# Cached attention of a decoder layer: two decoded rows share the 128 partitions, and one matmul sums the scores of both

## The chip, the cores and the metric

The kernel runs on one core of one Trainium2 chip. The metric is the device time in microseconds (us), the median over several executions. The engines named below are PE (TensorE, matmuls), DVE (VectorE), ACT (ScalarE), POOL (GpSimd) and SP (SyncE, which here only issues loads of weights). Each engine works through its own list of instructions in order and waits on semaphores for the others.

## The reference

One layer of a hybrid decoder is computed for a prompt of 256 tokens and for 8 decoded rows (`DEC_BATCH` 8, one token each). It projects the normalised input (RG-LRU and mLSTM heads), adds cross attention over 256 memory tokens in 4 heads of 512 features, and adds a SwiGLU block. The change is in the cross attention of the 8 decoded rows. Their keys and values are not computed but come from a cache:

```python
xq = (rmsnorm(x, g_xa) @ w_xa_q).reshape(B, L, XA_HEADS, XA_DH)
s = jnp.einsum('blhd,bmhd->bhlm', xq, mk.astype(dt)).astype(jnp.float32) * (XA_DH ** -0.5)
p = jax.nn.softmax(s, axis=-1).astype(dt)
o = jnp.einsum('bhlm,bmhd->blhd', p, mv.astype(dt)).reshape(B, L, D_MODEL)
x = x + o @ w_xa_o
...
xs, st_s = layer(xs, ..., cache_mem_k[l], cache_mem_v[l], *w)
```

For each of the 4 heads and each of the 8 rows this is a product of one query of 512 features with 256 cached keys, a softmax over the 256 scores, and a weighted sum of 256 cached values: 32 pairs of head and row, each with 512 KB of keys and 512 KB of values.

## The kernel before

**Layout.** Features lie on the 128 partitions, tokens along the free axis: 264 columns, 256 of the prompt and 8 decoded. A product with a weight matrix is a step of the list `steps`: SP loads the weights of the step (512 KB per half step) into `raw`, ACT rounds them to a high half, DVE subtracts to get the low half (`split_half`, tile `w`), and PE adds three products of halves (`mm3`). The program has 41 steps for `w_in`, 16 for `w_out`, 16 for `w_q` (queries), 32 for `w_k` and `w_v` (keys and values of the prompt, eight per head), 16 for `w_o` and then the SwiGLU block. Tile `w` has four buffers, which is two steps.

**Side work.** What is not a projection is written as generators (`side`, `pump`). After each step the main loop lets them issue instructions until estimates of the busy time of DVE and ACT reach that of PE. The order in which the instructions then stand on PE, DVE, ACT and POOL is set by a scheduler from priorities and a model of time; the splits of the weights have high priority. At run time the order on each engine is fixed.

**Cached attention before.** `evac_q` (line 1123) writes the queries of the decoded rows to `qsm`, partition by feature. When the fourth query step is evacuated, it starts two generators. `dec_k` (line 1142) goes over heads and rows. For each row POOL issues two loads of 512 KB from `kcT` and `vcT` into buffers of the pool `B` (26 buffers, lines 1151 and 1155). ACT multiplies the first quarter of the keys with the query column, DVE adds the other three with `scalar_tensor_tensor`, into the accumulator `dw`. ACT rounds the sum to `ds[0]` and POOL subtracts to get `ds[1]` (line 1162). At most two rows are under way (`NFL`). `dec_v` (line 1166) sums over the partitions with two matmuls whose weights are a 128x128 tile of ones (`onesr`), so that each partition gets the whole score row. DVE takes the maximum, ACT the exponential with its sum, and DVE multiplies the four quarters of the values with the probabilities and sums each (`accum_out` into `osm`). After 8 rows of a head DVE scales `osm`, and `attend` (line 1264) may use it: ACT and DVE split it into the tail columns of the operand of `w_o`.

**Order of the work.** The loads of keys and values, the subtractions on POOL and the stores of the prompt's keys and values share POOL's one list. The first step of `w_o` (`pe_o`) needs both generators to be done.

## Time and profile before

| what | us |
|---|---|
| median of 3 runs (1456.42 to 1458.74) | 1457.74 |
| the profiled execution, its own time | 1455.83 |
| its span, from first to last instruction | 1454.1 |
| PE busy in the span | 1439.2 |
| DVE busy | 1045.1 |
| ACT busy | 794.9 |
| POOL busy | 128.3 |

The query steps and the cached attention lie between about 375 and 652 us of the span. Busy shares are means over the span, and DVE's differs much between stages. The prediction reads that stretch by itself.

### The profile page before, as it was taken

What the parts mean: (1) busy time and instruction counts of PE and PEld (TensorE: products, weight loads), DVE (VectorE), ACT (ScalarE), POOL (GpSimd) and SP (SyncE); (2) the same over time, 40 slices, a digit from 0 to 9 for tenths busy, and PEclk for the clock granted to TensorE, in tenths of its full rate; (3) what the DMA queues carried; (4) which work ended last, traced back from release to release, by engine and by line L of the source; (5) the groups of instructions that cost most, each with busy time, mean ns of one, the idle gap of its engine ahead of it and who ended that gap; (6) DMA issues with size and microseconds to landing.
All of it is one profiled execution on the core that took longest, in us unless ns stands there. A gap on an engine that the chain in (4) does not pass through costs nothing.

```text
span 1454.1 us, 30126 instructions
## 1 busy us (share of the span) xinstructions
PE 1439.2 (99%) x12071; PEld 1415.5 (97%) x12071; DVE 1045.1 (72%) x1999; ACT 794.9 (55%) x1279; POOL 128.3 (9%) x204
## 2 busy tenths in 40 slices
PE   9999999999999999999999999999999999999997
PEld 8999999999999999999999999999999999999997
DVE  7966797898899999987675666555665655565564
ACT  7678685666556666655544444434444443444463
POOL 0001210000124343410000000000000000000000
PEclk9999999999999999999999999999999999999999
DMA  9645896557799877955555555555555555555563
GB/s 288 234 171 179 268 363 231 177 178 271 254 344 355 340 284 297 375 172 192 197 195 194 197 193 201 190 202 190 198 194 196 196 198 194 195 197 192 172 195 112
DMA packets 99757, 326.02 MB, mean 224 GB/s; under 512 B 10944, under 2 KB 19824, under 8 KB 99616
## 3 DMA queue, kind: packets, MB, share of 16 engines
q1 hardware_dynamic: 83616, 269.84, 52.8%
q0 software_dynamic: 15136, 53.16, 10.2%
q8 instruction: 94, 1.54, 0.4%
q10 hardware_dynamic: 864, 1.09, 0.2%
q14 instruction: 47, 0.39, 0.1%
HBM read 312.78 MB, written 11.28 MB: 223 GB/s over the span
## 4 chain that ended last, share of the span: by engine, by line
PE 94%; ACT 2%; DMA 1%; DVE 1%; issue 1%; SPq 0%; POOL 0%; DVEq 0%; POOLq 0%
PE mm L60 90%; PE ax L60 5%; DMA raw<-w_in 1%; ACT B L60 1%; DVE B L60 1%; DMA B<-scr 0%; ACT w L60 0%; DVE w L60 0%; ACT L60 0%; SPq L213 0%; ACT dw L60 0%; DVE ds L60 0%; SPq L1412 0%; DMA scr<-lt 0%; ACT t L60 0%
## 5 line engine op out<-in xcount | busy, mean ns | idle before, releaser
L60 PE MATMUL mm<-B,w 128*128 128x264 f32 (+1 forms) x10960 | 1281.2, 279 | 2.5 <-DVE w L60 2.1
L60 PEld LDWEIGHTS mm<-B,w 128*128 128x128 f32 x10960 | 1260.6, 189 | 10.7 <-DVE w L60 2.4
L60 DVE TENSOR_TENSOR w<-raw,w 128x1024 fp32r<-128x1024 f32 (+1 forms) x522 | 625.4, 1200 | 312.9 <-ACT w L60 312.2
L60 ACT ACTIVATE w<-raw 128x1024 fp32r<-128x1024 f32 (+1 forms) x522 | 536.0, 1028 | 531.8 <-PE mm L60 370.8
L60 PE MATMUL mm<-w,B 128*128 128x512 f32 x384 | 86.5, 380 | 0.0
L60 PEld LDWEIGHTS mm<-w,B 128*128 128x128 f32 x384 | 70.7, 189 | 9.4
L1494 POOL TENSOR_TENSOR B<-B,rstd 128x264 f32<-128x264 f32 x4 | 2.8, 741 | 802.8 <-ACT rstd L60 802.8
L60 DVE TENSOR_TENSOR t<-mm,rstd 128x264 f32<-128x264 f32 x96 | 41.4, 432 | 28.8 <-PE mm L60 28.7
L60 DVE SCALAR_TENSOR_TENSOR B<-B,dw 128x256 f32<-128x256 f32 x128 | 52.2, 461 | 3.2 <-ACT dw L60 2.9
L60 DVE TENSOR_TENSOR xres<-xres,mm 128x264 f32<-128x264 f32 (+1 forms) x81 | 34.2, 424 | 27.2 <-PE mm L60 27.1
L60 DVE SCALAR_TENSOR_TENSOR dw<-B,qsm,dw 128x256 f32<-128x256 f32 x96 | 48.6, 512 | 0.8
L60 PE MATMUL ax<-B,B 128*128 128x256 f32 (+3 forms) x288 | 46.0, 302 | 0.8 <-DVE B L60 0.8
L1162 POOL TENSOR_TENSOR ds<-dw,ds 128x256 fp32r<-128x256 f32 x32 | 36.8, 1151 | 106.9 <-ACT ds L60 104.7
L60 PEld LDWEIGHTS ax<-B,B 128*128 128x128 f32 x288 | 39.9, 191 | 3.0 <-DVE B L60 1.0
L60 ACT ACTIVATE B<-xres,vecs 128x264 fp32r<-128x264 f32 (+1 forms) x64 | 32.1, 502 | 3.5 <-DVE xres L60 1.6
L60 ACT ACTIVATE t<-xres 128x264 f32<-128x264 f32 (+1 forms) x53 | 21.0, 409 | 16.0 <-DVE xres L60 16.0
L1151 POOL DMA_DIRECT2D B<-kcT x32 | 17.4, 544 | 122.8 <-DVE B L60 109.7
L60 DVE SCALAR_TENSOR_TENSOR B<-xres,vecs,B 128x264 fp32r<-128x264 f32 x48 | 23.3, 488 | 4.3 <-ACT B L60 4.3
L60 ACT ACTIVATE dw<-B,qsm 128x256 f32<-128x256 f32 x32 | 16.2, 507 | 16.3 <-issue 6.4
L60 ACT ACTIVATE B<-t 128x264 fp32r<-128x264 f32 (+1 forms) x60 | 24.1, 409 | 1.7 <-DVE t L60 1.5
L60 ACT ACTIVATE dw<-B,B 128x128 f32<-128x128 f32 x64 | 20.9, 390 | 7.1 <-DMA B<-scr 6.3
L60 ACT ACTIVATE dw<-ax,dw 128x256 f32<-128x256 f32 x32 | 15.0, 470 | 17.7 <-DVE dw L60 14.0
(172 smaller groups left out, 691.2 us busy)
## 6 DMA issues: line engine op xcount, KB each, us to landing
raw<-w_gu SPq DMA_DIRECT2D x176, 512.0 KB, 3.6
raw<-w_d SPq DMA_DIRECT2D x80, 512.0 KB, 3.7
raw<-w_in SPq DMA_DIRECT2D x74, 512.0 KB, 5.2
raw<-w_out SPq DMA_DIRECT2D x32, 512.0 KB, 3.8
B<-kcT POOLq DMA_DIRECT2D x32, 512.0 KB, 8.2
raw<-w_q SPq DMA_DIRECT2D x32, 512.0 KB, 5.4
B<-vcT POOLq DMA_DIRECT2D x32, 512.0 KB, 9.1
raw<-w_k SPq DMA_DIRECT2D x32, 512.0 KB, 5.1
```

What stands on the lines that cost most here:

```text
L60: return f(*a, **k)
L1151: pool_e.dma_start(kc, kcT[h, b])
L1162: pool_e.tensor_sub(ws[:, 1], acc, ws[:, 0].bitcast(F32))
L1494: e.tensor_mul(st["y"](c), st["y"](c), r)
```

## The change

Two decoded rows now share the partitions: partitions 0 to 63 hold one row, 64 to 127 the other. The 128 partitions of the former layout do not fit 64, so the even and the odd features of each 128-block lie in two tiles. A load takes every second partition line of two rows of `kcT`, 128 lines of 4 KB as before, and writes all partitions. The keys of a pair of rows are two tiles, the values too.

- `onesr` becomes block diagonal: ones in the two 64x64 blocks, zero elsewhere. One pair of matmuls then sums the scores of two rows, each over its own half.
- Per pair of rows there are one ACT product and seven DVE products for the keys, one rounding, one subtraction, one pair of matmuls, one maximum, one exponential and eight products for the values.
- The tiles of keys and values come from a `Ring` of two buffers each. The load of the next tile stands behind the fourth product with the tile whose buffer it takes.
- `swap_q` brings the queries of a head into the new layout: a copy on POOL into `q3`, and four copies by DMA within SBUF into `q2`. `swap_o` takes the result back the same way, into `osm`. The loads of the four heads make 32 such small DMAs.

```diff
@@ -1129,70 +1129,123 @@
             dve.tensor_mul(qn["t"](j)[:, m:T], p2[:, 1, : T - m], rstd[:, m:T])
             dve.tensor_mul(qsm[:, j, :], p2[:, 1, T - m:], rstd[:, T:N])
             qn["n"] = j + 1
+            if j % 4 == 3:
+                swap_q(j // 4)
             if j == 3:
                 with tc.issue_after(st["split"].ins):
-                    act.activation(onesr, ones, AF.Copy)
+                    act.activation(onesr, ones, AF.Copy, scale=0.0)
+                    for part in (LOW, HIGH):
+                        act.activation(onesr[part, part], ones[part, part], AF.Copy)
                 st["dk"] = side(dec_k(), 5)
                 st["dv"] = side(dec_v(), 4)
         return f
 
     pairs = []
     infl = {"n": 0}
+    NB2 = NS // 2
+    q2 = const.tile([P, H, 2, 4, NB2], F32, name="q2")
+    q3 = const.tile([P, 2, 2, 4, NB2], F32, name="q3")
+    o2, o3 = q2, q3
+    LOW, HIGH = slice(0, 64), slice(64, P)
+
+    by_row = lambda x: x.rearrange("p c (b s) -> p s c b", s=2)
+
+    def swap_q(h):
+        pool_e.tensor_copy(q3[:, h % 2], by_row(qsm[:, 4 * h: 4 * h + 4, :]))
+        for q, part in enumerate((LOW, HIGH)):
+            for e in range(2):
+                pool_e.dma_start(q2[part, h, e], q3[e: P: 2, h % 2, q])
+
+    def swap_o(h):
+        rec = ssm[:, h, 0: NB2]
+        dve.reciprocal(rec, rec)
+        o = o2[:, h].rearrange("p g c b -> p (g c) b")
+        dve.tensor_mul(o, o, rec.rearrange("p (c b) -> p c b", c=1).to_broadcast([P, 8, NB2]))
+        for q, part in enumerate((LOW, HIGH)):
+            for e in range(2):
+                pool_e.dma_start(o3[e: P: 2, h % 2, q], o2[part, h, e])
+        pool_e.tensor_copy(by_row(osm[:, 4 * h: 4 * h + 4, :]), o3[:, h % 2])
+
+    class Ring:
+        def __init__(self, src):
+            self.t, self.at = [B([P, 4, T]), B([P, 4, T])], 0
+            self.src = src.rearrange("h b p c t -> h (b p) c t")
+            self.load()
+            self.load()
+
+        def load(self):
+            u = self.at
+            if u < H * NB2 * 2:
+                self.at = u + 1
+                b = u // 2 % NB2 * 2 * P + u % 2
+                pool_e.dma_start(self.t[u % 2], self.src[u // NS, b: b + 2 * P - 1: 2])
+
+        def __call__(self, j):
+            return self.t[j // 4][:, j % 4, :]
 
     def dec_k():
+        kr = Ring(kcT)
+        st["vr"] = Ring(vcT)
+        yield STEP
         for h in range(H):
             while qn["n"] < 4 * h + 4:
                 yield STEP
-            for b in range(NS):
+            for b in range(NB2):
                 while infl["n"] >= NFL:
                     yield STEP
                 infl["n"] += 1
-                kc = B([P, 4, T])
-                pool_e.dma_start(kc, kcT[h, b])
                 w = sb.tile([P, 264], F32, tag="dw", bufs=2, name=nm("dw"))
                 ws = sb.tile([P, 2, T], F32R, tag="ds", bufs=2, name=nm("ds"))
-                vc = B([P, 4, T])
-                pool_e.dma_start(vc, vcT[h, b])
                 acc = w[:, 0:T]
-                q = [qsm[:, 4 * h + c, b: b + 1] for c in range(4)]
-                act.activation(acc, kc[:, 0, :], AF.Copy, scale=q[0])
-                for c in range(1, 4):
-                    dve.scalar_tensor_tensor(acc, kc[:, c, :], q[c], acc, op0=OP.mult, op1=OP.add)
+                for j in range(8):
+                    q = q2[:, h, j // 4, j % 4, b: b + 1]
+                    if j == 0:
+                        act.activation(acc, kr(0), AF.Copy, scale=q)
+                    else:
+                        dve.scalar_tensor_tensor(acc, kr(j), q, acc, op0=OP.mult, op1=OP.add)
+                    if j % 4 == 3:
+                        kr.load()
+                    if j == 3:
+                        yield 1.0
                 act.activation(ws[:, 0], acc, AF.Copy)
                 pool_e.tensor_sub(ws[:, 1], acc, ws[:, 0].bitcast(F32))
-                pairs.append((h, b, w, vc, ws))
+                pairs.append((h, b, w, ws))
                 yield 1.1
 
     def dec_v():
         done, cur = 0, None
-        while done < H * NS:
+        while done < H * NB2:
             nxt = None
             if pairs:
                 nxt = pairs.pop(0)
                 ps = bank("ax")
-                pe.matmul(by2(ps[:, :T]), onesr, turn(nxt[4][:, 0]), start=True, stop=False)
-                pe.matmul(by2(ps[:, :T]), onesr, turn(nxt[4][:, 1]), start=False, stop=True)
+                pe.matmul(by2(ps[:, :T]), onesr, turn(nxt[3][:, 0]), start=True, stop=False)
+                pe.matmul(by2(ps[:, :T]), onesr, turn(nxt[3][:, 1]), start=False, stop=True)
                 nxt += (ps,)
             cur, todo = nxt, cur
             if todo is None:
                 yield STEP
                 continue
-            h, b, w, vc, _, ps = todo
+            h, b, w, _, ps = todo
             mx, p = w[:, T: T + 1], w[:, :T]
             dve.tensor_reduce(mx, ps[:, :T], axis=AX.X, op=OP.max)
             dve.tensor_scalar(mx, mx, -XSCALE, None, op0=OP.mult)
             act.activation(halves(p), unturn(ps[:, :T]), AF.Exp, scale=XSCALE, bias=mx,
                            accum_out=ssm[:, h, b: b + 1])
             yield 0.5
-            for c in range(4):
-                dve.scalar_tensor_tensor(vc[:, c, :], vc[:, c, :], 1.0, p, op0=OP.mult, op1=OP.mult,
-                                         accum_out=osm[:, 4 * h + c, b: b + 1])
+            for j in range(8):
+                v = st["vr"](j)
+                dve.scalar_tensor_tensor(v, v, 1.0, p, op0=OP.mult, op1=OP.mult,
+                                         accum_out=o2[:, h, j // 4, j % 4, b: b + 1])
+                if j % 4 == 3:
+                    st["vr"].load()
+                if j == 3:
+                    yield 1.0
             infl["n"] -= 1
             done += 1
-            if done % NS == 0:
-                dve.reciprocal(ssm[:, h, :], ssm[:, h, :])
-                for c in range(4):
-                    dve.tensor_mul(osm[:, 4 * h + c, :], osm[:, 4 * h + c, :], ssm[:, h, :])
+            if done % NB2 == 0:
+                swap_o(h)
+                yield STEP
                 st["dh"] = h + 1
             yield STEP
 
```

**What moves.** Three places are shown, one on POOL and two on DVE. Names carry buffer numbers here.

POOL before, in the query steps: `ds` is the rounded score sum, `B_...` the tiles of keys (`kcT`) and values (`vcT`) of one row.

```order
L1162 TENSOR_TENSOR ds_633_5239<-dw_632_5238,ds_633_5239 128x256
L1151 DMA B_648_5386<-kcT 128x1024
L1155 DMA B_651_5390<-vcT 128x1024
L1151 DMA B_658_5470<-kcT 128x1024
L1155 DMA B_661_5474<-vcT 128x1024
L1151 DMA B_668_5554<-kcT 128x1024
L1155 DMA B_671_5558<-vcT 128x1024
L1162 TENSOR_TENSOR ds_650_5389<-dw_649_5388,ds_650_5389 128x256
```

The loads of three rows, into six different buffers, stand ahead of the next subtraction.

POOL now, in the same steps: `B_627` and `B_628` are the two buffers of the key ring (even and odd features), `B_629` and `B_630` those of the value ring.

```order
L1181 DMA B_627_5233<-kcT 128x1024
L1181 DMA B_629_5237<-vcT 128x1024
L1181 DMA B_630_5238<-vcT 128x1024
L1181 DMA B_628_5234<-kcT 128x1024
L1211 TENSOR_TENSOR ds_654_5476<-dw_653_5475,ds_654_5476 128x256
L1181 DMA B_627_5233<-kcT 128x1024
L1154 COPY q3_116<-qsm_112 128x32
L1157 DMA q2_115<-q3_116 64x16 x4
L1181 DMA B_628_5234<-kcT 128x1024
L1211 TENSOR_TENSOR ds_667_5633<-dw_666_5632,ds_667_5633 128x256
```

Each load goes into a buffer that was just read, and the small DMAs of `swap_q` stand between loads.

DVE now, the third and the fourth pair of rows: `dw_653` and `dw_666` are their accumulators, `w_...` the splits of weights, `B_660` and `qsm` the evacuation of a query step.

```order
L60 SCALAR_TENSOR_TENSOR dw_653_5475<-B_628_5234,q2_115,dw_653_5475 128x256
L60 TENSOR_TENSOR B_660_5562<-mm_670_5648,rstd_94 128x132
L60 TENSOR_TENSOR B_660_5562<-mm_670_5648,rstd_94 128x124
L60 TENSOR_TENSOR qsm_112<-mm_670_5648,rstd_94 128x8
L60 SCALAR_TENSOR_TENSOR dw_666_5632<-B_627_5233,q2_115,dw_666_5632 128x256
L60 TENSOR_TENSOR w_675_5717<-raw_665_5623,w_675_5717 128x8x128
L60 TENSOR_TENSOR w_682_5804<-raw_671_5697,w_682_5804 128x8x128
L60 SCALAR_TENSOR_TENSOR dw_666_5632<-B_628_5234,q2_115,dw_666_5632 128x256
```

The first row is the last read of the odd key tile for one pair, the last row its first read for the next pair. The load of that tile has to be issued and to land in between, while DVE has six instructions to do.

DVE now, the last two pairs of the fourth head, in the steps for the prompt's keys and values: `dw_849` and `dw_878` are their accumulators.

```order
L60 SCALAR_TENSOR_TENSOR dw_849_7250<-B_628_5234,q2_115,dw_849_7250 128x256
L60 TENSOR_TENSOR w_910_7723<-raw_900_7632,w_910_7723 128x1024
L60 SCALAR_TENSOR_TENSOR dw_878_7475<-B_627_5233,q2_115,dw_878_7475 128x256
L60 TENSOR_TENSOR w_918_7776<-raw_904_7698,w_918_7776 128x1024
L60 SCALAR_TENSOR_TENSOR dw_878_7475<-B_628_5234,q2_115,dw_878_7475 128x256 x2
```

Again the odd key tile is read for the last time in the first row and for the next pair in the last, with three instructions between.

## The prediction

> **What bounds the kernel now.** I read the engines' busy time first, then the busy time of the stretch that the change touches, then what PE waited for, then the groups and the order in time inside the stretch.
>
> ```profile
> PE 1439.2 (99%) x12071; PEld 1415.5 (97%) x12071; DVE 1045.1 (72%) x1999; ACT 794.9 (55%) x1279; POOL 128.3 (9%) x204
> ...
> 380.00:640.00 260.00, 260.00 (x1730) 242.96 (x1729) 248.74 (x639) 164.50 (x306) 95.55 (x130) 1.00 0.85 317
> 400.00:420.00 20.00, 20.00 (x181) 20.00 (x180) 19.64 (x58) 11.14 (x19) 5.78 (x10) 1.00 0.90 338
> 800.00:900.00 100.00, 100.00 (x892) 100.00 (x891) 60.20 (x74) 44.83 (x55) 0.00 (x0) 1.00 0.56 195
> ...
> PE mm L60 <- DVE w L60: 2.1, 2, 1.9
> PE ax L60 <- ACT w L60: 2.1, 3, 1.5
> ```
>
> The rows of stretches give, after the length, the busy us of PE, weight loads, DVE, ACT and POOL, then the granted clock, the DMA share and GB/s. PE is busy for all of 380 to 640 us at full clock, and DVE for 248.74 of 260, so DVE has only 11.3 us to spare there. A busy PE might still be paced by others, because the ends of matmuls are modelled. So I count: 181 matmuls in 20 us while the cached attention runs, against 892 in 100 us, or 178 in 20, in the SwiGLU block, where DVE is 60% busy. PE is not held back. In the whole run PE waited 2.1 us at most for any one partner; asked for 380 to 655 us alone, the view has no row. The kernel is therefore bound by PE, and DVE is close behind just here. A gain has to take matmuls away; work taken from ACT or POOL gains nothing by itself.
>
> **What the change takes away.**
>
> ```profile
> L60 PE MATMUL ax<-ds,onesr 128*128 128x256 f32 x64 | 17.1, 277 | 0.0
> L60 DVE SCALAR_TENSOR_TENSOR dw<-B,qsm,dw 128x256 f32<-128x256 f32 x96 | 48.6, 512 | 0.8
> L60 DVE SCALAR_TENSOR_TENSOR B<-B,dw 128x256 f32<-128x256 f32 x128 | 52.2, 461 | 3.2 <-ACT dw L60 2.9
> L1162 POOL TENSOR_TENSOR ds<-dw,ds 128x256 fp32r<-128x256 f32 x32 | 36.8, 1151 | 106.9 <-ACT ds L60 104.7 <-PE mm L60 2.0
> L60 ACT ACTIVATE dw<-B,qsm 128x256 f32<-128x256 f32 x32 | 16.2, 507 | 16.3 <-issue 6.4 <-DVE B L60 4.7 <-ACT w L60 2.9
> L60 DVE TENSOR_REDUCE dw<-ax 128x1 f32<-128x256 f32 x32 | 13.3, 416 | 0.3 <-PE ax L60 0.2
> L60 DVE TENSOR_SCALAR dw<-dw 128x1 f32<-128x1 f32 x32 | 4.7, 147 | 0.2
> ...
> 444.18 0.27 PE L60 MATMUL ax<-ds,onesr 128*128 128x256 f32 x1
> 444.29 3.17 PE L60 MATMUL mm<-B,w 128*128 128x264 f32 x23
> ...
> 394.83 1.22 DVE L60 TENSOR_TENSOR w<-raw,w 128x1024 fp32r<-128x1024 f32 x1
> 395.97 0.48 DVE L60 SCALAR_TENSOR_TENSOR dw<-B,qsm,dw 128x256 f32<-128x256 f32 x1
> 396.37 0.48 DVE L60 TENSOR_TENSOR B<-mm,rstd 128x132 f32<-128x132 f32 x2
> 396.76 0.15 DVE L60 TENSOR_TENSOR qsm<-mm,rstd 128x8 f32<-128x8 f32 x1
> 396.84 0.47 DVE L60 SCALAR_TENSOR_TENSOR dw<-B,qsm,dw 128x256 f32<-128x256 f32 x1
> 397.23 0.41 DVE L60 TENSOR_REDUCE dw<-ax 128x1 f32<-128x256 f32 x1
> ```
>
> The groups give count, busy us and mean ns, then idle time before them. PE loses 32 of the 64 matmuls on `onesr`. One lasts 277 ns but matmuls overlap: the next starts 0.11 us later (444.18 to 444.29). That is 32 x 0.11 = **3.5 us**, all on the path that sets the end. PE had no wait in the stretch, so no more than this can be won.
>
> DVE's instructions overlap too, so I use distances of starts: 1.14 us for a split of weights (394.83 to 395.97), 0.40 for a key product, 0.47 for an evacuation of queries with `qsm` (396.37 to 396.84), 0.33 for a maximum by the same reading. DVE gets 16 key products more (+6.4 us), and loses 16 maxima and 16 small scalings (16 x (0.33 + 0.15) = -7.7 us) and 12 small products on `osm`, at most 12 x 0.15 = -1.8. That is 3 us less, and none of it on the path. ACT loses 16 products of 0.507 us and 16 roundings and exponentials; PE never waited for it there, so it counts nothing. POOL loses 16 subtractions, 16 x 1.151 = 18.4 us, also off the path. But it may let DVE run faster: key products average 512 ns against 470 to 480 in the rows above, so 96 x 0.035 = 3.4 us, and the value products and splits look alike. I take 5 us of DVE time for half of POOL's subtractions gone, between 0 and 10. So DVE has 11.3 + 3 + 5 = 19 us to spare over the stretch.
>
> [...]
>
> **What it adds: hops through DMA.** `swap_q` is a copy on POOL, four DMA issues and their landing; `swap_o` the same backwards.
>
> ```profile
> L1494 POOL TENSOR_TENSOR B<-B,rstd 128x264 f32<-128x264 f32 x4 | 2.8, 741 | 802.8 <-ACT rstd L60 802.8
> scr<-lt POOLq DMA_DIRECT2D x1, 32.0 KB, 1.8
> o_h<-hlast POOLq DMA_DIRECT2D x1, 36.0 KB, 6.0
> 386.64 0.53 POOL L1151 DMA_DIRECT2D B<-kcT  x1
> 381.49 1.06 POOL L1162 TENSOR_TENSOR ds<-dw,ds 128x256 fp32r<-128x256 f32 x1 [25.96 <-ACT ds L60]
> 390.19 0.38 PE L60 MATMUL ax<-ds,onesr 128*128 128x256 f32 x2
> L60 DVE TENSOR_TENSOR osm<-osm,ssm x16: 151/156/164, 445.9 to 637.1; 128x8 f32<-128x8 f32 x16
> L60 DVE TENSOR_TENSOR B<-osm,B x16: 154/160/164, 533.3 to 652.0; 128x8 fp32r<-128x8 f32 x16
> ```
>
> A hop takes at most 0.74 + 4 x 0.53 + landing of 1.8 to 6.0, so 4.7 to 8.9 us. The first head's `swap_q` is covered by PE's own order: before, the first pair of halves was ready at 382.55 (381.49 + 1.06) and used at 390.19, 7.6 us later. The later heads' hops run while the head before is worked on. `swap_o` is covered by the distance from `osm` to its use, 14.9 us at the last head (637.1 to 652.0). Price if the cover is gone: 8.9 - 7.6 = 1.3 us once. I take 0.
>
> **What it adds: loads that cannot run ahead.** Before, POOL issued the loads of three rows at once into free buffers. Now a tile is loaded only when it has been read, and DVE, which holds the splits of weights, waits in order if it is late.
>
> ```profile
> DMA to landing us min/median/max: 3.8/8.2/13.9
> B<-kcT POOLq DMA_DIRECT2D x1, 512.0 KB, 4.6
> B<-kcT POOLq DMA_DIRECT2D x1, 512.0 KB, 4.0
> B<-kcT POOLq DMA_DIRECT2D x1, 512.0 KB, 6.1
> B<-kcT POOLq DMA_DIRECT2D x1, 512.0 KB, 13.9
> 414.48 0.88 POOL L1162 TENSOR_TENSOR ds<-dw,ds 128x256 fp32r<-128x256 f32 x1
> 417.07 0.27 PE L60 MATMUL ax<-ds,onesr 128*128 128x256 f32 x1
> 419.98 0.74 POOL L1162 TENSOR_TENSOR ds<-dw,ds 128x256 fp32r<-128x256 f32 x1
> 422.24 0.27 PE L60 MATMUL ax<-ds,onesr 128*128 128x256 f32 x1
> ```
>
> The first row is the time from issue to landing of the 32 key loads. The next are single ones, issued at 336.65, 429.72, 385.55 and 387.68 us: 4.0 to 6.1 with none of their own kind ahead, 13.9 as the fifth of a burst of six. The ring sends one or two at a time, so I take 5.0, nearest to the single ones, with 3.8 and 8.2 as ends.
>
> Against it stands DVE's work between the last read of a tile and the next. At the fourth pair of the order shown that is 0.47 + 0.40 + 2 x 1.14 = 3.2 us, so DVE waits 1.8 us. At the last pair it is 2 x 1.14 + 0.40 = 2.7 us, a wait of 2.3. Added up in the same way, the 15 gaps of the odd key tile are 4.0, 11.6, 3.2, 8.3, 8.7, 6.6, 6.5, 5.6, 7.7, 5.0, 9.3, 5.7, 5.7, 14.8 and 2.7; those of the even one have only one (4.4) below 5, those of the values none. With 5.0 DVE waits about 1.0 + 1.8 + 2.3 = 5.1 us, well inside the 19 us, so the weights do not run dry. But behind the waiting product stand the accumulator, its rounding on ACT, POOL's subtraction and the two matmuls, in PE's fixed order. Before, PE came to the second of these 1.7 and 1.5 us after POOL had ended (415.36 to 417.07, 420.72 to 422.24). With 1.5 us of slack, PE loses 0 + 0.3 + 0.8 = **1.1 us**.
>
> The sum against the profiled execution's 1455.83 us: -3.5 + 1.1 = -2.4, so 1453.4. The median of the runs is 1.9 above that execution; I carry the difference over: 1457.74 - 2.4 = **1455.3 us**, 0.16% less.
>
> **The rivals.**
>
> *No wait at all.* If loads land in about the shortest time seen, 3.8 us, the waits are 0.6 and 1.1 at two places, below the slack, and the whole 3.5 us remains: 1454.2. For it: the DMA engines are less pressed without bursts. Against: one load of the four single ones took 6.1. [...] The trace has no key load below 3.8.
>
> *The ring is too short.* If landings stay at their median of 8.2, the odd key tile alone is late ten times, by 4.2 + 5.0 + 1.6 + 1.7 + 2.6 + 0.5 + 3.2 + 2.5 + 2.5 + 5.5 = 29.3 us. DVE can make up 18 to 19, so PE runs dry of weights for about 11 us: 1457.74 - 3.5 + 11 = 1465 us, slower than before. At 7.0 the sum is 18 us, just what DVE can make up, so this mechanism decides from a mean landing of about 7 us on. For it: the DMA share of 0.85 in the stretch, and SP's weights go on beside it. Against: half of that pressure was the bursts.
>
> *The freed time goes elsewhere.* The matmuls are gone, but the first hop is late by 1.3 us, or PE is paced by DVE after all: 1456 to 1457.7. The count of matmuls above speaks against it.
>
> **How the numbers follow.** Forecast 0.38 (its own range 1454.2 to 1457.5), no wait 0.20, ring too short 0.32, time gone elsewhere 0.10. A change below 0.2%, 2.9 us, can hardly be told from none here, so faster means under 1454.8 and slower above 1460.7. Faster: 0.20 and 0.14 of the forecast's 0.38. Slower: 0.30 of the 0.32. The rest, 0.36, is between. Eight times in ten the time should lie from 1453.7, just under the whole gain, to 1466, just over the price of late loads.
>
> **What would show it.** Right: 32 matmuls on `onesr`, no wait of PE between 380 and 655 us above 1 us, key loads landing in about 5 us, short idle times of DVE or ACT before key products that name the load, DVE below 248 us of 260. Wrong: idle times of DVE that name key loads adding up to more than 19 us, PE waiting for `w`, or idle time of PE before matmuls on `onesr` of several us.

## The result, and the profile after

The changed kernel takes **1483.39 us** in the median of 4 runs (1480.59 to 1484.29), against 1457.55 for the kernel before beside it: a ratio of 1.0176, with a 95% interval of 1.0164 to 1.0189. I had forecast 1455.3 and a range up to 1466. The change costs some 26 us. The profiled execution took 1484.29 us, with a span of 1482.6. Two executions far outside the others are left out everywhere, one of the run with half of the bytes (1659.93 us, at a granted clock of 0.849) and one of the kernel before (3078.39 us).

First the engines' busy time on the page of the changed kernel, then the same three stretches as before and three short ones. After the length stand the busy us of PE, weight loads, DVE, ACT and POOL, the granted clock, the DMA share and GB/s:

```profile
PE 1445.4 (97%) x12039; PEld 1416.0 (96%) x12039; DVE 1046.6 (71%) x1971; ACT 772.9 (52%) x1217; POOL 133.1 (9%) x228
```

```profile
380.00:640.00 260.00, 237.19 (x1537) 216.63 (x1536) 229.59 (x577) 127.25 (x219) 93.66 (x145) 0.99 0.86 292
400.00:420.00 20.00, 20.00 (x181) 20.00 (x180) 19.33 (x61) 9.38 (x13) 6.90 (x12) 1.00 0.94 299
800.00:900.00 100.00, 100.00 (x891) 100.00 (x890) 61.33 (x76) 45.20 (x57) 0.00 (x0) 1.00 0.60 195
560.00:580.00 20.00, 14.19 (x87) 12.69 (x87) 15.48 (x42) 10.62 (x22) 6.55 (x12) 0.96 0.76 267
580.00:600.00 20.00, 20.00 (x109) 17.89 (x108) 19.13 (x41) 10.64 (x23) 10.50 (x17) 0.96 0.93 317
620.00:640.00 20.00, 16.10 (x93) 14.31 (x92) 15.71 (x45) 8.41 (x20) 6.86 (x9) 0.91 0.67 207
```

The 32 matmuls are gone (12071 to 12039), and the SwiGLU stretch is as it was. The loss lies where the cached attention runs: PE, busy for all of 380 to 640 us before, is now idle for 22.8 of the 260. DVE has no more to do than before (1046.6 us in the whole span against 1045.1), but within these 260 us it gets less of it done, 229.59 us against 248.74: it waits as well. Next, what PE waited for between 380 and 655 us (total us, times, longest); before, this view had no row:

```profile
PE ax L60 <- ACT ds L60: 6.5, 7, 1.8
PE mm L60 <- DVE w L60: 5.9, 3, 4.2
PE mm L60 <- DVE t L60: 3.9, 1, 3.9
PE ax L60 <- POOL ds L1211: 3.4, 4, 1.6
PE ax L60 <- DVE B L60: 1.7, 1, 1.7
PE ax L60 <- DVE dw L60: 1.3, 1, 1.3
```

The rows add up to 22.7 us. Most of them stand for two things: PE comes to the matmuls on `onesr` before their operand `ds` is ready (9.9 us), and the weights `w` come too late (5.9 us). The waits for `t` and `dw` (5.2 us) come right after waits of DVE for key loads, of 5.54 us until 623.25 and of 2.44 us until 538.03; the one for `B` (1.7 us) I did not trace. PE's idle time over the whole span grew by 22.3 us (from 14.9 to 37.2). Its busy time grew too, by 6.2 us with 32 matmuls fewer; the lower clock that was granted gives some 3 us of that by my estimate (last section), and the rest stays open. The waits lead back to one place, as the groups on the page show (busy, mean ns, then idle time and what ended it):

```profile
L60 DVE SCALAR_TENSOR_TENSOR dw<-B,q,dw 128x256 f32<-128x256 f32 x112 | 58.0, 522 | 25.0 <-DMA B<-kcT 19.8
L60 DVE SCALAR_TENSOR_TENSOR B<-B,dw 128x256 f32<-128x256 f32 x128 | 54.0, 483 | 1.3 <-DMA B<-vcT 1.3
L60 ACT ACTIVATE dw<-B,q 128x256 f32<-128x256 f32 x16 | 8.1, 509 | 41.4 <-DMA B<-kcT 21.2
...
B<-kcT POOLq DMA_DIRECT2D x32, 512.0 KB, 7.2
B<-vcT POOLq DMA_DIRECT2D x32, 512.0 KB, 6.1
```

DVE waited 19.8 us for key loads, and ACT another 21.2 before the first product of a pair. A key load lands 7.2 us after its issue in the median, not the 5.0 I took. How such a wait reaches PE shows at PE's longest one: DVE waits for a key load until 569.49, the splits of weights behind it start late, and PE waits about as long for `w` (start, us, instruction, and in brackets the idle time before it and what ended it):

```profile
569.49 0.48 DVE L60 SCALAR_TENSOR_TENSOR dw<-B,q,dw 128x256 f32<-128x256 f32 x1 [4.01 <-DMA B<-kcT]
...
577.53 5.65 PE L60 MATMUL mm<-B,w 128*128 128x256 f32 x23 [4.21 <-DVE w L60]
```

The timeline of POOL shows a second delay, ahead of the issue:

```profile
423.86 0.53 POOL L1181 DMA_DIRECT2D B<-kcT  x1 [6.97 <-DVE dw L60]
424.40 2.87 POOL L1211 TENSOR_TENSOR ds<-dw,ds 128x256 fp32r<-128x256 f32 x1
427.23 0.58 POOL L1181 DMA_DIRECT2D B<-kcT  x1
432.28 1.59 POOL L1154 COPY q<-qsm 128x32 f32<-128x32 f32 x1 [4.47 <-DVE dw L60]
434.16 2.12 POOL L1157 DMA_DIRECT2D q<-q  x4 [0.30 <-POOL q L1154]
436.27 0.54 POOL L1181 DMA_DIRECT2D B<-kcT  x1
```

The load at 427.23 follows directly on a subtraction that took 2.87 us, for which PE waited 1.65 us as well; the load at 436.27 stands behind a copy and the four issues of a `swap_q`. DVE's key product for the load of 423.86 started at 430.52 after 3.83 us of idle time:

```profile
430.52 0.48 DVE L60 SCALAR_TENSOR_TENSOR dw<-B,q,dw 128x256 f32<-128x256 f32 x1 [3.83 <-DMA B<-kcT]
```

This is the fourth pair, for which I had worked out a wait of 1.8 us.

### The profile page after: what moved, and what is told of

Its sections match the earlier page's. It is cut to its first block, busy times and chain, and to the rows that moved or that the text cites. A ratio compares the mean times of both kernels' runs of the same rounds, so it can differ in the third digit from the quotient of the medians.

```text
span 1482.6 us, 29952 instructions
## 1 busy us (share of the span) xinstructions
PE 1445.4 (97%) x12039; PEld 1416.0 (96%) x12039; DVE 1046.6 (71%) x1971; ACT 772.9 (52%) x1217; POOL 133.1 (9%) x228
## 4 chain that ended last, share of the span: by engine, by line
PE 57%; issue 1%; DVE 1%; DMA 1%; POOL 0%; ACT 0%; DVEq 0%; POOLq 0%
PE mm L60 56%; PE ax L60 1%; DMA B<-kcT 1%; DVE B L60 0%; DVE w L60 0%; POOL B L1181 0%; ACT w L60 0%; DVE c L60 0%; DVE dw L60 0%; DVEq L1632 0%; DVE t L60 0%; ACT t L60 0%; DVE xres L60 0%; ACT c L60 0%; POOLq L1181 0%
## 5 line engine op out<-in xcount | busy, mean ns | idle before, releaser
L60 DVE SCALAR_TENSOR_TENSOR dw<-B,q,dw 128x256 f32<-128x256 f32 x112 | 58.0, 522 | 25.0 <-DMA B<-kcT 19.8
L60 DVE TENSOR_TENSOR t<-mm,rstd 128x264 f32<-128x264 f32 x96 | 41.3, 431 | 28.6 <-PE mm L60 28.5
L60 ACT ACTIVATE dw<-B,q 128x256 f32<-128x256 f32 x16 | 8.1, 509 | 41.4 <-DMA B<-kcT 21.2
L60 PE MATMUL ax<-B,w 128*128 128x264 f32 x144 | 22.0, 280 | 2.4 <-ACT w L60 2.4
L60 ACT ACTIVATE t<-t 128x264 f32<-128x264 f32 (+1 forms) x53 | 21.6, 407 | 3.2 <-DVE t L60 3.2
```

Of the source, the lines that this page charges most:

```text
L60: return f(*a, **k)
```

## The experiments

Three theories stood at the start. A: the ring's loads come late, and ACT, DVE and PE wait behind them. B: the hops of q and of the output, with their copies, hold up POOL. C: the layout itself, a chain of eight products cut in two pieces, delays the splits of weights. The edits are shortened to the lines that matter. In what follows a kernel's time is its median, and "before" is the kernel before, run beside it (1456.8 to 1457.1 us). Where it matters I give the end as well: the time from the last VectorE instruction to the end of the span, 4.5 us in both kernels (here 1445.45 + 4.16 = 1449.61 and a span of 1454.1 before).

### Taking the loads away

Loads only once:

```diff
-            if u < H * NB2 * 2:
+            if u < 2:
```

> The changed kernel with the two key tiles and the two value tiles loaded once, at the start, and never again: 120 of the 128 slots of 512 KB are left out, so the cached attention works on the wrong rows from the second pair on; every product, sum and hop is still issued. Theory A (the 26 us are waits for ring loads that come too late, and what stands behind them on DVE, ACT and PE): the waits for B<-kcT and B<-vcT go to under 3 us together and the time comes to 1450 to 1457 us. Theory B (the hops of q and o and what they hold up on POOL): 1478 us or more. Theory C (the new layout itself, a chain of eight products cut in two pieces, is what delays the weights' splits): 1475 us or more.

(There are 64 loads, of which 60 are left out; the count in the expectation is wrong.) Measured: **1461.36 us**, ratio 1.003 (1.0017 to 1.0043). PE is busy for 258.1 of the 260 us again, and yet the time lies above A's range. The reason is at the end of the program, on DVE's timeline:

```profile
1445.88 3.82 DVE L60 TENSOR_TENSOR B<-B,ax 128x264 f32<-128x264 f32 x11
```

DVE ends at 1449.70, as before, but the span runs to 1458.8: an end of 9.1 us instead of 4.5. Without these 4.6 us the run stands at 1456.8, level with before. So about 26 us hang on the loads. Theories B and C fall as main causes, since hops and layout are all in this run.

Half of the bytes of each load after the first two of a ring:

```diff
-                pool_e.dma_start(self.t[u % 2], self.src[u // NS, b: b + 2 * P - 1: 2])
+                pool_e.dma_start(self.t[u % 2][:, 0:2] if u > 1 else self.t[u % 2],
+                                 self.src[u // NS, b: b + 2 * P - 1: 2, 0:2] if u > 1 else self.src[u // NS, b: b + 2 * P - 1: 2])
```

> The changed kernel with every ring load after the first two of each ring cut to half of its bytes, features 0 and 1 of a tile; features 2 and 3 of the cached rows are left out (the first rows' stand in their place). Same number of loads, same points of issue, same order. Theory A with the landing as its main term: the landing falls from 7.2 us to about 5, by the ratio of the 256 KB and 512 KB weight loads (2.7 and 3.9 us), and the time to 1462 to 1474 us. Rival P (POOL's order): 1478 us or more, with landings shorter but waits for B<-kcT still above 30 us.

Measured: **1463.75 us** (a single run). The key loads of this run, from the view of the tile `kcT`, and PE's waits in the stretch:

```profile
DMA to landing us min/median/max: 2.8/4.5/7.8
```

```profile
PE ax L60 <- ACT ds L60: 2.6, 2, 1.6
PE mm L60 <- DVE w L60: 1.6, 2, 1.3
PE ax L60 <- POOL ds L1212: 1.2, 3, 0.7
```

With the landing at 4.5 instead of 7.2 us, 19.6 of the 26 us are gone, and the time is in A's range. DVE's and ACT's waits for key loads fall from 41.0 to 4.1 us. That is not the landing alone, though. The expectation says that the order stays, but the scheduler set another one: between the first head's hops and the first subtraction POOL has three key loads here and two in the change. The DMA share of the stretch falls too, from 0.86 to 0.76. And at a landing even below my 5.0 the kernel is still 7 us slower than before.

Loads of 4 KB after the first two of each ring, and the same without hops (by the edit of the run without hops further down):

```diff
-                pool_e.dma_start(self.t[u % 2], self.src[u // NS, b: b + 2 * P - 1: 2])
+                c, n = (slice(0, 4), T) if u < 2 else (slice(0, 1), 8)
+                pool_e.dma_start(self.t[u % 2][:, c, 0:n], self.src[u // NS, b: b + 2 * P - 1: 2, c, 0:n])
```

> The changed kernel with every ring load after the first two of each ring cut to 8 numbers of a row, 4 KB in all; the cached rows after the first are left out (the products run over what stands there). Same loads, points of issue and order as the change. The landing falls to 2 to 4 us. If what stays at half the bytes (7.9 us over the span before) is landing too, the time comes to 1454 to 1459 us; if it is POOL's order, where a load waits for its tile ahead of a subtraction or a copy, 1460 to 1465 us.

> Tiny ring loads as in the run that gave 1462.6 us, and also no hops: the halves of q and of the output are copied in place by one VectorE copy a head, so POOL makes neither copies nor 32 small transfers. The cached rows after the first and the swap of halves are left out. If the hops' place in POOL's order is what remains (PE waited 4.5 us for POOL's subtractions there), 1454 to 1457.5 us. If it is the ring, whose loads wait on POOL until a tile is read whatever their size, 1460 to 1464 us, with PE ax <- POOL ds still above 3 us.

Measured: **1462.58 us** with hops (1.0039, 1.0024 to 1.0055) and **1459.86 us** without (1.0023, 1.0014 to 1.0032); the median landing of key loads is 3.1 and 2.9 us. The first fell among the times for POOL's order, the second between its two ends. In the first, POOL's timeline around the hops of an output, and what PE did:

```profile
494.52 2.06 POOL L1166 DMA_DIRECT2D q<-q  x4 [0.23 <-DVE q L60]
500.13 1.66 POOL L1167 COPY osm<-q 128x32 f32<-128x32 f32 x1 [3.55 <-DMA q<-q]
501.75 0.82 POOL L1212 TENSOR_TENSOR ds<-dw,ds 128x256 fp32r<-128x256 f32 x1
502.51 0.57 POOL L1182 DMA_DIRECT2D B<-kcT  x1
```

```profile
502.62 0.38 PE L60 MATMUL ax<-ds,onesr 128*128 128x256 f32 x1 [1.61 <-POOL ds L1212]
```

POOL waits 3.55 us for the hops to land, copies, and only then subtracts: PE waits 1.61 us. Without hops, PE's waits for POOL's subtractions fall from 4.5 to 1.8 us, and the time by 2.7. So the ladder is: 19.6 us from the change to half the bytes, 1.2 from there to 4 KB, 2.7 without hops, and 3 above before that are left even then. The order of the instructions differs at every step (four key loads stand ahead of the first subtraction with 4 KB), so these are prices of a kernel with its order, and not of one cause each. In the last 3 us the gain of the 32 matmuls is lost as well; what takes it I could not resolve further.

Loads of neighbouring rows, to see what the stride costs:

```diff
-                b = u // 2 % NB2 * 2 * P + u % 2
-                pool_e.dma_start(self.t[u % 2], self.src[u // NS, b: b + 2 * P - 1: 2])
+                b = u % NS * P
+                pool_e.dma_start(self.t[u % 2], self.src[u // NS, b: b + P])
```

> The changed kernel with every ring load taking 128 neighbouring rows of 4 KB (512 KB in one piece) instead of every second row out of 256; so a pair gets the wrong rows, same bytes, same order. If the stride makes the landing long, kcT lands in about 5 us in place of 7.2 and the time falls to 1462 to 1474 us. If a load of 512 KB takes its 7 us in this stage whatever its rows, 1480 to 1486 us and a median landing of 6.5 to 7.5 us; I expect this.

Measured: **1478.60 us** (2 runs, 1477.58 to 1479.61), between the two expectations, with a median landing of 6.7 us. Here the instructions do stand in the order of the change. The runs of the change lie all above these, 1480.59 to 1484.29, so the stride may be worth some 0.5 us of landing and 5 us of time; most of the 7 us is there without it.

### Is it the ring, or the layout?

The old layout with a ring of two:

```diff
-                kc = B([P, 4, T])
-                pool_e.dma_start(kc, kcT[h, b])
+                kc = kr.t[b % 2]
...
+                kr.load()
                 act.activation(ws[:, 0], acc, AF.Copy)
```

(and the same for the values)

> The kernel before, with its own layout (one row per chain of four products, 64 matmuls on onesr, no hops), but its keys and values loaded into a ring of two tiles each, the next load issued when a row's products have read a tile. Nothing is left out. Theory A (a ring of two tiles, loaded after its last reader, is what costs): 1470 to 1490 us, with 15 us or more of waits for B<-kcT. Rival D (a ring costs only in the new layout, since there a chain of eight products stands between two loads of the same tile and ACT's splits stand behind its first product): 1456 to 1462 us.

Measured: **1467.59 us**, 1.0071 (1.0056 to 1.0086): 10.5 us slower than before, between the two expectations, and not by the way expected. No engine waited for a key load; PE waited for POOL:

```profile
PE ax L60 <- POOL ds L1176: 4.6, 6, 2.2
```

The ring costs without the layout too, but only 10.5 us against 26. PE's waits in the stretch come to 6.2 us of them; the rest I did not trace. In this run key loads landed in 5.5 us.

The new layout with fresh tiles, as the kernel before did it:

```diff
-        kr = Ring(kcT)
-        st["vr"] = Ring(vcT)
...
+                kr, vr = Pair(kcT, h, b), Pair(vcT, h, b)
```

> The new layout without the ring: each pair takes two key tiles and two value tiles from the pool of 26 when it begins, and loads them then, as the kernel before did for each row; two pairs may be in flight. Nothing is left out. Theory A (the ring's late loads): 1453 to 1458 us, the layout alone being worth about 32 matmuls of 0.11 us, 3.5 us. A rival to it (the layout with eight tiles instead of four takes buffers that other steps need): 1460 us or more with waits for buffers, not for loads. Theory B (the hops): 1478 us or more.

Measured: **1473.37 us**, 1.0117 (1.0102 to 1.0132). The rival was right about the time but not about the place. One wait of PE makes up most of it, and it is for POOL. POOL's timeline ahead of it, and PE:

```profile
454.69 0.54 POOL L1166 DMA_DIRECT2D q<-q  x1 [1.64 <-DVE w L60]
456.97 0.53 POOL L1166 DMA_DIRECT2D q<-q  x1 [1.75 <-DMA B<-kcT]
...
472.35 0.54 POOL L1157 DMA_DIRECT2D q<-q  x1 [2.03 <-DMA B<-vcT]
...
474.06 0.74 POOL L1201 TENSOR_TENSOR ds<-dw,ds 128x256 fp32r<-128x256 f32 x1
```

```profile
474.85 0.58 PE L60 MATMUL ax<-ds,onesr 128*128 128x256 f32 x1 [8.84 <-POOL ds L1201]
```

Eight hops of 4 KB, put one behind the other by the scheduler, take 18.2 us to issue (454.69 to 472.89), nearly each after a wait of 2 us that the landing of a 512 KB load ended. The subtraction stands behind them.

Four key tiles, two value tiles:

```diff
-            self.t, self.at = [B([P, 4, T]), B([P, 4, T])], 0
+            self.t, self.at, self.n = [B([P, 4, T]) for _ in range(n)], 0, n
...
-        kr = Ring(kcT)
-        st["vr"] = Ring(vcT)
+        kr = Ring(kcT, 4)
+        st["vr"] = Ring(vcT, 2)
```

> The changed kernel with four key tiles in the ring in place of two; the value ring stays at two. Nothing is left out. A key load is then issued a whole pair (some 11 us) earlier than it is needed. Theory A (late ring loads): the waits of DVE and ACT for B<-kcT, 19.8 and 21.2 us, fall under 6 us in all and the time to 1454 to 1462 us. Theory B (the hops): 1478 us or more, since hops and their order on POOL stay. Theory C (the layout): 1478 us or more.

Measured: **1464.20 us**, 1.0047 (1.003 to 1.0063), above A's range by 2 us. All 41 us of waits for key loads are gone, although these land in 7.6 us. In their place the value ring comes next:

```profile
DVE B L60 <- DMA B<-vcT: 7.2, 5, 3.4
```

The ring of two, reloaded in halves:

```diff
-                pool_e.dma_start(self.t[u % 2], self.src[u // NS, b: b + 2 * P - 1: 2])
+                pool_e.dma_start(self.t[e][:, c], self.src[u // 16, b: b + 2 * P - 1: 2, c])
...
-                    if j % 4 == 3:
+                    if j % 2 == 1:
                         kr.load()
```

> The changed kernel with the same two tiles in each ring, but loaded in halves of two features, 256 KB each: a half is loaded again after its own two products, two products before the whole tile is free. 256 loads instead of 128... of half the size; nothing is left out and no memory is added. Theory A (late loads; a load is late by its landing, 7.2 us, less the work between last reader and next reader): two products of 0.52 us more room and a shorter landing, so the waits for B<-kcT fall from 41 us to under 20 and the time to 1460 to 1472 us. Rival P (not the landing but the order on POOL, where a load stands behind other loads' waits and subtractions): twice the issues on POOL make it no better, 1480 to 1490 us.

(It is 128 loads instead of 64.) Measured: **1469.25 us**, 1.0075 (1.0058 to 1.0092), in A's range: waits for key loads of 6.1 and 5.7 us instead of 19.8 and 21.2. And 5.2 us of this time are again the end: 9.7 us instead of 4.5.

The changed kernel without hops, the halves copied in place:

```diff
-        pool_e.tensor_copy(q3[:, h % 2], by_row(qsm[:, 4 * h: 4 * h + 4, :]))
-        for q, part in enumerate((LOW, HIGH)):
-            for e in range(2):
-                pool_e.dma_start(q2[part, h, e], q3[e: P: 2, h % 2, q])
+        dve.tensor_copy(q2[:, h], by_row(qsm[:, 4 * h: 4 * h + 4, :]))
```

(and `swap_o` likewise)

> The changed kernel without the small transfers inside the chip: the halves of q and of the output are copied in place by one VectorE copy instead of swapped (32 hops, 8 POOL copies left out, so each row meets the wrong half of its query). Loads and ring as in the change. Theory A (late ring loads): 1474 to 1483 us, since only the loads that stood behind the hops' issues on POOL come earlier, about 2 us at each of some 4 places. Theory B (the hops): 1455 to 1462 us. Theory C (the layout): 1480 us or more.

Measured: **1488.89 us**, 1.022 (1.0205 to 1.0236), 5.5 us slower than with hops: above the ranges of A and B, and in that of C alone ("1480 us or more"). C does not follow from it, since the same layout with loads made once is level with before. The scheduler set another order, in which ACT waited 28.9 us for key loads and DVE 15.8. It says that hops are not the main cause, and no more; the nearest to a price of theirs is the pair with tiny loads.

The order of the instructions thus differs from run to run. But in the runs of the new layout whose ring POOL loads, here and below, the time goes with the waits of DVE and ACT for key loads: 38.9 to 44.7 us of waits in the three that take 1478 to 1489 us (the change, neighbouring rows, no hops), and at most 11.8 in the others, none of them above 1470.4 us.

### Loads on another queue

SP issues the ring's loads. `Ring` takes here the number of tiles, the pieces in which a tile is loaded, and the queue:

```diff
-        kr = Ring(kcT)
-        st["vr"] = Ring(vcT)
+        kr = Ring(kcT, 2, 1, sp)
+        st["vr"] = Ring(vcT, 2, 1, sp)
```

(in the second run `Ring(kcT, 4, 1, sp)` and `Ring(vcT, 2, 2, sp)`, in the third `3, 2, sp` for both)

> The changed kernel, rings of two whole tiles, with the 64 ring loads issued by SP instead of POOL, in program order between the weight loads. Nothing is left out. A ring load then stands no more behind POOL's subtractions and swap copies, but the weight loads stand behind ring loads that wait for their tile. Theory A with the landing as main term (7.2 us, and 512 KB moved beside the weights): the waits for B<-kcT stay above 25 us and the time at 1474 to 1486 us. Rival P (POOL's order is the main term): waits under 15 us, 1462 to 1470 us. Above 1486 us it is the weights that come late: then PE waits for w more than the 7.9 us of the change.

> As the run before, but the ring loads (whole tiles for the keys, halves for the values) are issued by SP. Nothing is left out. Theory A: 1453 to 1459 us, since no load is late and nothing stands in front of the subtraction on POOL; this is the run in which the 32 matmuls could show as 3.5 us less than before. Rival: the weight loads behind ring waits come late, PE waits for w over 8 us, 1462 to 1475 us.

> Rings of three tiles for keys and for values, in halves, issued by SP; two more tiles than the change, as with four and two. Nothing is left out. Theory A: a half is then issued six products before its reader where two tiles in halves gave six less four; 1453 to 1460 us. Rival as in the run before: weights held up on SP, 1462 to 1475 us.

Measured: **1497.02 us** for the two whole tiles, **1494.74** for four key tiles, **1480.06** for rings of three in halves (ratios 1.0275, 1.0259 and 1.0159). The rival with the weights named the right mechanism three times, and its range was too low in the last two; some 4.3 us of each of the three times are again the end (8.7 to 8.8 us), without which the third would be at 1475.8. In the first, DVE and ACT wait only 10.3 us for key loads; whether that is POOL's order gone or only the slower pace of the rest, the run can't tell. The weight loads stand behind the ring loads that wait for their tile (79.9 us on SP's queue for DVE's key products in this first run), and PE runs dry, as its waits show:

```profile
PE mm L60 <- ACT w L60: 14.6, 9, 4.0
PE mm L60 <- DVE w L60: 8.7, 12, 1.9
```

A key load lands in 7.2 us from SP's queue just as from POOL's.

### A better version, and the end of the program

Four key tiles and two value tiles, in halves, on POOL:

```diff
-        kr = Ring(kcT)
-        st["vr"] = Ring(vcT)
+        kr = Ring(kcT, 4, 2, pool_e)
+        st["vr"] = Ring(vcT, 2, 2, pool_e)
```

> The new layout with four key tiles and two value tiles, both loaded in halves of 256 KB on POOL. Nothing is left out. With four key tiles whole the time was 1464.2 us with 7.2 us of DVE waits for B<-vcT and none for B<-kcT; with halves and two tiles 1469 us with 11.8 us of waits for kcT and none for vcT. Theory A: neither load is waited for, and 1456 to 1461 us are left. Rival P: 128 issues of 0.54 us and their waits in POOL's order hold up the subtraction that PE waits for: 1463 to 1470 us with PE ax <- POOL ds above 4 us.

Measured: **1461.78 us**, 1.0035 (1.0021 to 1.0049). PE is busy for 257.7 of the 260 us, and waits for POOL's subtraction not at all, yet the time misses A's range. Again it is the end; DVE's last row of this run and the span of 1460.4 give 9.8 us:

```profile
1447.50 3.14 DVE L60 TENSOR_TENSOR B<-B,ax 128x264 f32<-128x264 f32 x9
```

Long ends (8.7 to 9.8 us) were seen in the runs in which POOL issues 99, 103 or 227 transfers, the short one of 4.5 with 131 or 163. By the records of the traces the last long instruction on POOL is a closing `DRAIN`, which took 10.9 to 11.9 us in the six runs with a long end and 4.0 to 6.5 us in all others (4.82 us before, 6.53 in the change). Two kernels were to tell whether that number sets it, by transfers of 2 KB on POOL while it has nothing to do:

```diff
+        if i == 130:
+            for k in range(32):
+                pool_e.dma_start(q3[:, 0, 0, 0, :], vec[:, 0:4] if k else raws[i][0][:, 0:4])
```

> Four key tiles and two value tiles in halves on POOL, as in the run that gave 1461.8 us, with 32 transfers of 2 KB added on POOL in the feed-forward stretch: 259 issues instead of 227. Nothing is left out. The runs so far show the long end at 99, 103 and 227 issues and the short one at 131 and 163, so it may begin anew every 128; then 259 gives the short end, 4.5 us, and 1456 to 1457.5 us although there is more to do. If it grows with the number, the end is longer than 9.8 us and the time 1462 to 1465 us.

> The kernel before, with 96 transfers of 2 KB added on POOL's queue in the feed-forward stretch, one after the other into a tile that nobody reads, while POOL has nothing to do (803 us of it). Nothing is left out. POOL then issues 227 transfers, as the run with key ring of four in halves did, in place of 131. If the time between the last store and the end follows that number, the stretch from the last VectorE instruction to the end grows from 4.5 us to 9.8 and the time to 1461.5 to 1462.8 us. If it belongs to the attention's change, 1456 to 1458 us.

Measured: four keys in halves with 32 more, **1455.60 us** (10 runs, 1455.19 to 1457.92), ratio to before 0.9993 (0.9983 to 1.0002). The kernel before with 96 more, **1457.12 us**, ratio 1.000 (0.999 to 1.001). In the first the end is short again, 1446.15 + 4.16 to a span of 1454.8:

```profile
1446.15 4.16 DVE L60 TENSOR_TENSOR B<-B,ax 128x264 f32<-128x264 f32 x12 [0.93 <-PE ax L60]
```

The second refutes my rule: 227 issues, and an end of 4.5 us. Issues after the attention made the end short in one kernel, and did not make it long in the other. What sets the length of the `DRAIN` and of the end stays open.

On the kernel with the 32 more transfers, a third value tile, and output hops that write to `osm` without a copy:

```diff
-        st["vr"] = Ring(vcT, 2, 2, pool_e)
+        st["vr"] = Ring(vcT, 3, 2, pool_e)
```

```diff
-                pool_e.dma_start(o3[e: P: 2, h % 2, q], o2[part, h, e])
-        pool_e.tensor_copy(by_row(osm[:, 4 * h: 4 * h + 4, :]), o3[:, h % 2])
+                pool_e.dma_start(by_row(osm[e: P: 2, 4 * h: 4 * h + 4, :])[:, q], o2[part, h, e])
```

> As the run before, with a third value tile (seven tiles in the rings, three more than the change). Nothing is left out. If the 2.4 us of waits for B<-vcT and the 2.4 us of PE idle time that are left come from the value ring, 1453.5 to 1456 us, below both kernels; if the seven tiles are missing to the steps that share the pool, 1457 to 1462 us.

> Four key tiles and two value tiles in halves, with the 32 idle transfers that made the end short (1455.6 us), and the output's hops writing straight into osm, four bytes at a time, so that POOL need not wait for their landing to copy. Nothing is left out. If POOL's wait for the hops held PE up there, 1453.5 to 1455 us, below the kernel before by over 0.2%; if small pieces land later than the cover of 14.9 us at the last head, or nothing waited, 1455 to 1460 us.

Measured: **1470.33 us** with the third value tile (1.0092, 1.0077 to 1.0107), slower than either expectation; PE waited 5.1 us once for a VectorE instruction on the tile of queries and outputs, and 2.7 for weights. **1456.61 us** with hops that need no copy (1.000, 0.9991 to 1.0009): no gain. The best version is thus four key tiles and two value tiles in halves with the short end, at 1455.6 us: 28 us below the change, and not to be told from the kernel before.

## Why the prediction failed, point by point

**What bounds the kernel: right.** PE did, and 22.7 us of the 28.5 between the two spans are waits of PE in 380 to 655 us.

**The gain of 32 matmuls x 0.11 us: right in size, not won.** With loads made once, by the records of the trace, 12 fewer matmuls on `onesr` had been issued by the 3500th matmul on a bank `mm`. Its distance to the 2750th is 93.4 us there and 94.8 before: 1.3 us for 12, or 0.11 each. Of the 3.5 us in all, the median of the best version is 1.35 us below before, which its interval (0.9983 to 1.0002) does not tell from none.

**DVE's 19 us to spare: wrong in one term and in its use.** The 5 us that fewer subtractions on POOL were to give did not come: key products took 512 ns in the mean before and 522 after. And spare time could not be saved up here: a wait of DVE delayed the splits behind it, and PE ran out of weights a few us later (569.49 and 577.53 above), whatever DVE could do at another place. That is why PE waited 5.9 us for `w`, although DVE was busy for only 229.59 of 260 us. The step mattered: at the measured landing of 7.2 us my list of gaps gives DVE 19.8 us of waits, about what I took as spare, so by it the weights would hardly have run dry.

**The hops at cost 0: wrong by 2.7 us.** I had set each hop against the first use of its own data. That cover held. But a copy that waited on POOL (3.55 us in the run with 4 KB loads) also held what was queued behind it, the next subtraction and the next key load, and I named neither. The 2.7 us hold for loads of 4 KB, and with another order of instructions.

**The landing of 5.0 us: the step that failed first.** I took the value nearest to single loads, with 3.8 and 8.2 as ends; it came out at 7.2. My choice of single loads was too narrow: the same profile has key loads that POOL issued one at a time in the query steps, at 413.93, 419.43 and 437.96 us, the last with no other key load under way, and they landed in 9.0, 8.6 and 7.4 us. In the change the DMA share of the stretch stayed as high as before (0.86 against 0.85), so "half of that pressure was the bursts" did not hold. This step alone does not give the 26 us, however. With 7.2 in place of 5.0, my own way of counting (each wait less 1.5 us of slack) makes PE lose 8.0 us at the odd key tile and 1.3 at the even one, so 1457.74 - 3.5 + 9.3 = 1463.5 us. The other 20 us come from the steps on DVE's spare time, on the waits and on the hops; how they divide, no run shows, since the edits that took one of them away also changed the order.

**The waits: right on DVE, missing on ACT and POOL.** By my list of gaps DVE waits 18 us at a landing of 7.0, and 19.8 at 7.2; it waited 19.8. That the sums agree so well is luck in part: the list has nine waits and the trace seven, some of them longer by delays of the issue that the list leaves out. And I had found one late load of the even tile, which ACT reads first, and there were six, 21.2 us. The gaps came from the order of the instructions without any delay of the issue; on POOL an issue was held up by as much as a subtraction of 2.87 us. And DVE's spare time did not pay for ACT's waits, since the rounding of the weights and of `ds` stood behind them.

**PE's slack of 1.5 us** was taken at two matmuls and used once for each wait. In the change PE waited at eleven places for `ds`, 9.9 us.

**The rival "the ring is too short"** had the mechanism, and its point of decision, a landing of about 7 us; the rivals without a wait and with the freed time going elsewhere fell with the 22.7 us. Its price of 11 us was for a landing of 8.2; at 7.2 the same sum gives about 1. The price was too low for two reasons: ACT's part was missing, and 18 us of DVE's waits were taken as made up.

## What to carry to other kernels

A ring that was loaded again only after its last reader turned the landing of a transfer, which free buffers had hidden, into a wait on every engine that reads it: 19.8 us on DVE and 21.2 on ACT here. Count the wait on each of them, and take the landing under the load of that stage (here 7.2 us), not that of single transfers in a profile (4.0 to 6.1 us for the ones I took). A transfer that waited for a buffer or for other data delayed what stood behind it in POOL's order, with fresh tiles a subtraction of 0.74 us for which TensorE waited 8.84. Spare time of an engine, summed over a stretch, did not pay for a wait at one place of it: PE waited 5.9 us for `w` although DVE was busy for only 229.59 of 260 us. Where a scheduler sets the order, compare the order of two kernels before an edit is given a price.

## What the runs showed of the hardware

- The landing of a ring load beside the weights, medians of the keys: 512 KB in 7.2 us (6.7 with neighbouring rows), 256 KB in 4.5 and 4 KB in 3.1. Size and traffic fall together in these three: where all bytes were loaded, in halves of 256 KB on POOL, a half took 5.7 to 6.7 us, at a DMA share of 0.88 to 0.90 in place of 0.76. The shortest landings of the three were 3.5, 2.8 and 1.8 us.
- After the two longest waits of PE between 380 and 655 us, 4.21 and 3.89 us, the granted clock fell: 0.96, 0.96 and 0.91 in the three stretches of 20 us above, 0.56 and 0.59 in the 2 us from 578 and from 580. PE had 9 matmuls in each of these two, and 14 of the same shape in the 2 us from 582, at 1.00. In the rest of that part of the span, with waits of up to 1.8 us, the clock stayed at 1.00; earlier, a wait of 1.88 us until 126.55 stood ahead of 0.50 in the 2 us from 128. With fresh tiles the 20 us from 460, with the wait of 8.84 us in them, show 0.75. By my estimate from the three stretches the lower clock adds some 3 us (0.04 + 0.04 + 0.09 of 20) to the 22.7 of waits.
- The span ran on for 4.5 us after DVE's last instruction in most runs, and for 8.7 to 9.8 in six of them. These 4 to 5 us, three times the difference between the best version and the kernel before, can hide or feign the effect of an edit far away.
- A subtraction of 128x256 on POOL took 0.74 to 2.87 us, and the longest held up a key load by nearly all of it.
